# Eight of eleven down projection steps by seven products instead of seven, with smaller scratch

## The chip, the cores and the metric

The kernel runs on one core of a Trainium2 chip. The time is device microseconds of one execution. Engines are named as in the profile: PE (TensorE matmul), PEld (its weight loads), DVE (VectorE), ACT (ScalarE), POOL (GpSimd) and SP (SyncE, which here only issues DMAs).

## The reference

One decoder layer on 272 positions (16 meta tokens and 256 tokens) of width 2048, float32:

```python
h = h + concat(retention_heads, mlstm_heads) @ w_out
u = rmsnorm(h, norm_ffn)
up = causal_dwconv(u @ w_up, ffn_conv_w, ffn_conv_b)      # 2 x 5632 wide, 3 taps
gate, val = split(up, [FFN_DIM])
h = h + (silu(gate) * val) @ w_down                       # 5632 x 2048
out = rmsnorm(h, norm_final)[:, N_META:]
```

The change lies in the last product, `(silu(gate) * val) @ w_down`, and in what is prepared for it.

## The kernel before

**Precision.** Every large product is taken in three matmuls: an operand x is kept as hi = x rounded to fp32r and lo = x - hi, and hi*hi + lo*hi + hi*lo are summed in PSUM. For a weight tile this means a DMA into a `wraw` buffer (4 of them), a cast on ACT into `whi` and a subtraction on DVE into `wlo` (5 each; `load_w`, L114 to L124).

**Stages in time.** Input projections and the two kinds of heads; `w_out` (L630 to L638); then twice (two halves of the FFN rows) an up projection and a down projection. An up projection makes 22 pairs of 128-row tiles (gate and value), each by `project`, `conv3`, Silu and a multiplication (L770 to L788). The 22 tiles of a half are 11 steps of the down projection, two tiles each.

**Down projection.** Per half it runs two blocks, `b` = 0 and 2 (L915): output columns of strips b and b+1, 512 each. A block has four PSUM sums `cs[tt, j]` (token half tt, strip j; pool `at`, four buffers) and four more, `ps` (pool `mm`, four buffers).

- A *plain* step (`product`, L813) loads both strips' weights and makes 2 strips x 2 token halves x 2 row tiles x 3 = 24 matmuls of 512 columns.
- A *fast* step (`seven`, L833) treats the step as a 2x2 block product (activation blocks A11, A12, A21, A22 by row tile and token half; weight blocks B11 to B22 by row tile and strip) and makes seven products of 3 matmuls, 21, by Winograd's form of Strassen's scheme. The activation sums S1 to S4 are made on POOL in the up stage (L802 to L805), the weight sums in `seven` and earlier. Seven steps of eleven are fast: `FAST` (L593); in the last block of all, the two in `BOTH` are plain.

**Weight sums.** One of them, T2 = B22 - B12 + B11, is made in advance for each fast step: class `Early` (L599) loads three 512-wide weight blocks on POOL's queue into a home, two DVE sums follow some projections later (L615, L616), and the result goes to DRAM (`kept`, L617). `seven` then loads it (L840) with three blocks from `wd7` (L841) into one of two raw places in `hT` (`left`, in turn), makes two more sums (L844, L845; their results take `wraw` buffers) and casts and splits four groups. `wd7` is a copy of the weights in the order in which `seven` wants them.

**Ends of a block.** After the last fast step `share` (L877 on) turns the four `ps` into four x tiles and adds each to `hn` in SBUF by an accumulating DMA from POOL's queue (`onto`, L878). After the last step the four `cs` are copied by ACT into x tiles (L951) and sent the same way. x tiles are slices of `x5`, which has five; the copies use 4, 3, 1, 0 and `share` uses 0 to 3. `seven` of the next block's first fast step casts only behind the last of these copies (`emptied`). In the last block the sums are added to `hn` by DVE instead (`add`), with an order of steps of its own, and four plain steps of strip 3 are kept for the end.

**Order.** Within an engine instructions run in program order, which a planner makes from the order of emission, its own estimates of time and the `issue_after` rules. An engine, and SP's queue of DMA issues too, stands still while its next instruction waits for a semaphore.

The two lines on which the ends of a block turn:

```python
x6, x7, x5, x1 = (x_tile(i) for i in range(4))          # share
x = x_tile((4, 3, 1, 0)[2 * j + n])                     # copies of cs
```

Of the kernel before, what the change touches and what calls it, by code (L numbers as in the profile page):

```python
# [83 lines left out]
def trunk(ctx: ExitStack, tc: tile.TileContext, io, out: bass.AP):  # L84
    nc = tc.nc
# [5 lines left out]
    wpool = ctx.enter_context(pool("wpool", 1, side="left"))  # L91
# [501 lines left out]
    FAST = [1, 2, 3, 5, 6, 7, 8]  # L593
# [5 lines left out]
    class Early:  # L599


        def __init__(self, b, q, home, after, pace=None):

            self.home, self.age = home, 0
            self.kept = dram.tile([P, 512], F32, name=f"kept{b}_{q % NQD}", bufs=1)
# [6 lines left out]
        def finish(self, after):  # L612
            t = self.home[:, 0, :]
            with tc.issue_after(after.ins):
                nc.vector.tensor_tensor(out=t, in0=self.home[:, 1, :], in1=t, op=ALU.subtract)  # L615
            nc.vector.tensor_tensor(out=t, in0=self.home[:, 2, :], in1=t, op=ALU.add)  # L616
            nc.gpsimd.dma_start(self.kept, t)  # L617

    early, running = {}, []
    ahead = [(0, q) for q in FAST[:5]]  # L620
# [3 lines left out]
    begins = [1, 4, 6, 8, 10]  # L624
# [39 lines left out]
    x5 = midp.tile([P, 5, 512], F32, name="x5")  # L664
    pace = midp.tile([P, 1], F32, name="pace")

    def x_tile(i):
        return x5[:, i, :]
# [8 lines left out]
    def conv3(ps, f, name):  # L677
# [3 lines left out]
        o = wk2.tile([P, SEQ], F32, name=name)  # L681
# [62 lines left out]
    for half in range(2):  # L744
        units = [(b, q) for b in (0, 2) for q in FAST if (half, b) != (1, 2) or q not in BOTH]
        homes = [left[0][:, 0:3, :], left[1][:, 0:3, :], x5[:, 1:4, :]]
        if half == 0:
            units = units[len(ahead):]
            begins = [2 + 4 * i for i in range(9)]
            homes = 9 * [homes[2]]  # L750
# [18 lines left out]
        for jj in range(NHF):  # L769
# [27 lines left out]
            else:  # L797
# [5 lines left out]
                nc.gpsimd.tensor_tensor(out=sums[:, S3, :], in0=e11, in1=e21, op=ALU.subtract)  # L803
# [28 lines left out]
        def seven(b, q, cs, ps, first, last, after, norm):  # L832
# [7 lines left out]
            nc.sync.dma_start(raw[:, 0, :], early[b, q])  # L840
            nc.sync.dma_start(raw[:, 1:4, :], io["wd7"][b // 2, half * NQD + q][:, 1:4, :])  # L841
            ta, tb = (wpool.tile([P, 2, 512], F32, name="wraw", bufs=4) for _ in range(2))

            nc.vector.tensor_tensor(out=ta, in0=raw[:, 0:1, :].to_broadcast([P, 2, 512]), in1=raw[:, 1:3, :], op=ALU.subtract)  # L844
            nc.vector.tensor_tensor(out=tb[:, 0, :], in0=raw[:, 3, :], in1=raw[:, 0, :], op=ALU.subtract)  # L845
            copied = None
            for w, to in (
                (raw[:, 2:4, :], ((S4, cs[0, 1], False, False), (A12, cs[0, 0], False, False))),
                (raw[:, 0:2, :], ((S2, ps[2], first, last), (A11, ps[0], first, last))),
                (ta, ((S3, ps[1], first, last), (S1, ps[3], first, last))),  # L850
                (tb[:, 0:1, :], ((A22, cs[1, 0], False, False),)),
# [217 lines left out]
```

## Time and profile before

| what | value |
| --- | --- |
| median of 3 runs | 1207.14 us (1205.92 to 1208.45) |
| the profiled execution, its own time | 1207.7 us |
| its span, first to last instruction | 1205.9 us |
| granted PE clock | 0.999 |
| down projection, first half | about 718 to 833 us of the span |
| down projection, second half | about 1084 us to the end |

The profile has a page of fixed parts (busy time by engine, the span in 40 slices, DMA queues, the chain of work that ended last) and views that answer to questions: busy time by stage, groups of instructions by line, instructions in order of time with the idle time before them and what ended it, and DMA issues in a stretch with their median time to landing. In a row such as `wlo<-wraw,whi 128x1024` the names are the program's tiles, with out before the arrow.

### The profile page before, as it was taken

To read this page: it belongs to the slowest core of one execution; us is meant where nothing else is said; L and a number is where in the kernel's file an instruction comes from. 1 tells how busy PE (TensorE), PEld (TensorE's weight loads), DVE (VectorE), ACT (ScalarE), POOL (GpSimd) and SP (SyncE) were. 2 spreads that over 40 slices of the span, in tenths; PEclk is the share of its full clock that TensorE was granted. 3 is DMA by queue.
4 is the path that set the end of the run, shared out by engine and by line. 5 is a ranking of instruction groups with operands and counts; after the bars stand their busy time and mean duration, and the time that the engine had idled before them with its cause. 6 is when DMAs were issued, how large, how long until landed. Compare 5 with 4: busy or idle time off the path is not lost.

```text
span 1205.9 us, 22794 instructions
## 1 busy us (share of the span) xinstructions
PE 1194.6 (99%) x8956; PEld 1151.2 (95%) x8956; DVE 971.5 (81%) x1444; ACT 709.5 (59%) x963; POOL 162.8 (14%) x223
## 2 busy tenths in 40 slices
PE   9999999999999999999999999999999999999997
PEld 9999999999999999999999998878999999998886
DVE  8968788766775966789889879897788778789897
ACT  8747656655656646555555557664555555556664
POOL 0100001111110311021122100202022112100232
PEclk9999999999999999999999999999999999999999
DMA  8765555666565965766766834959787777755956
GB/s 278 269 212 164 170 184 170 197 183 192 169 192 165 349 200 175 252 220 212 253 219 214 279 117 175 278 177 276 284 251 255 223 240 249 261 176 211 274 181 186
DMA packets 83004, 263.27 MB, mean 218 GB/s; under 512 B 14672, under 2 KB 18896, under 8 KB 82768
## 3 DMA queue, kind: packets, MB, share of 16 engines
q1 hardware_dynamic: 71952, 223.85, 57.0%
q0 software_dynamic: 10368, 37.11, 10.1%
q8 instruction: 70, 1.15, 0.4%
q10 hardware_dynamic: 576, 0.85, 0.2%
q14 instruction: 38, 0.31, 0.1%
HBM read 243.42 MB, written 11.27 MB: 211 GB/s over the span
## 4 chain that ended last, share of the span: by engine, by line
PE 96%; DMA 2%; DVE 1%; ACT 0%; issue 0%; SPq 0%; DVEq 0%; ACTq 0%
PE mmps L130 26%; PE mmps L131 25%; PE mmps L133 25%; PE atps L827 2%; PE atps L828 2%; PE atps L830 2%; PE mmps L860 2%; PE mmps L862 2%; PE mmps L859 2%; PE atps L862 1%; PE atps L860 1%; PE atps L859 1%; DMA hn<-x 1%; PE atps L379 1%; DMA hT<-in_wd 1%; PE atps L371 0%
## 5 line engine op out<-in xcount | busy, mean ns | idle before, releaser
L121 ACT CAST whi<-wraw 128x1024 fp32r<-128x1024 f32 x352 | 369.3, 1050 | 342.0 <-PE mmps L131 228.7
L123 DVE TENSOR_TENSOR wlo<-wraw,whi 128x1024 fp32r<-128x1024 f32 x352 | 432.3, 1230 | 72.5 <-ACT whi L121 70.0
L130 PE MATMUL mmps<-uh,whi 128*128 128x258 f32 x1408 | 346.1, 283 | 0.0
L131 PE MATMUL mmps<-ul,whi 128*128 128x258 f32 x1408 | 346.0, 283 | 0.0
L130 PEld LDWEIGHTS mmps<-uh,whi 128*128 128x128 f32 x1408 | 267.6, 190 | 0.1
L131 PEld LDWEIGHTS mmps<-ul,whi 128*128 128x128 f32 x1408 | 267.1, 190 | 0.1
L130 PE MATMUL mmps<-xh,whi 128*128 128x272 f32 (+2 forms) x864 | 219.8, 288 | 0.0
L131 PE MATMUL mmps<-xl,whi 128*128 128x272 f32 (+2 forms) x864 | 218.3, 286 | 0.0
L133 PE MATMUL mmps<-uh,wlo 128*128 128x258 f32 x1408 | 196.5, 282 | 0.0
L133 PEld LDWEIGHTS mmps<-uh,wlo 128*128 128x128 f32 x1408 | 179.9, 189 | 0.0
L131 PEld LDWEIGHTS mmps<-xl,whi 128*128 128x128 f32 x864 | 162.8, 188 | 0.0
L130 PEld LDWEIGHTS mmps<-xh,whi 128*128 128x128 f32 x864 | 162.5, 188 | 0.1
L133 PE MATMUL mmps<-xh,wlo 128*128 128x272 f32 (+2 forms) x864 | 126.7, 285 | 0.0
L133 PEld LDWEIGHTS mmps<-xh,wlo 128*128 128x128 f32 x864 | 114.2, 188 | 0.0
L680 DVE TENSOR_TENSOR cu<-mmps,rstd 128x258 f32<-128x258 f32 x88 | 37.4, 425 | 55.3 <-PE mmps L133 54.8
L764 ACT CAST whi<-hT 128x1024 fp32r<-128x1024 f32 x52 | 53.6, 1052 | 27.2 <-PE atps L828 7.3
L766 DVE TENSOR_TENSOR wlo<-hT,whi 128x1024 fp32r<-128x1024 f32 x52 | 62.1, 1220 | 4.9 <-ACT whi L764 3.7
L131 PE MATMUL mmps<-mixl,whi 128*128 128x258 f32 x256 | 63.0, 283 | 0.0
L130 PE MATMUL mmps<-mixh,whi 128*128 128x258 f32 x256 | 62.4, 282 | 0.0
L764 ACT CAST whi<-wraw 128x1024 fp32r<-128x1024 f32 (+1 forms) x52 | 43.0, 838 | 16.8 <-PE mmps L860 6.8
L766 DVE TENSOR_TENSOR wlo<-wraw,whi 128x1024 fp32r<-128x1024 f32 (+1 forms) x52 | 52.2, 1037 | 0.6 <-PE mmps L862 0.2
L827 PE MATMUL atps<-whi,mh 128*128 128x512 f32 (+1 forms) x132 | 50.9, 387 | 1.3 <-ACT whi L121 1.1
(280 smaller groups left out, 1700.1 us busy)
## 6 DMA issues: line engine op xcount, KB each, us to landing
wraw<-in_wu SPq DMA_DIRECT2D x176, 512.0 KB, 4.4
wraw<-in_wi SPq DMA_DIRECT2D x108, 512.0 KB, 4.1
hT<-in_wd SPq DMA_DIRECT2D x26, 768.0 KB, 4.7
wraw<-in_wd SPq DMA_DIRECT2D x36, 512.0 KB, 4.7
wraw<-in_wo SPq DMA_DIRECT2D x32, 512.0 KB, 4.2
x<-in_wd POOLq DMA_DIRECT2D x13, 768.0 KB, 7.0
hn<-x POOLq DMA_DIRECT2D x27, 256.0 KB, 7.9
hT<-kept SPq DMA_DIRECT2D x26, 256.0 KB, 2.9
```

Source lines behind the costliest of these rows:

```text
L121: nc.scalar.copy(hi, raw)
L123: nc.vector.tensor_tensor(out=lo, in0=raw, in1=hi.bitcast(F32), op=ALU.subtract)
L130: nc.tensor.matmul(ps, hi[:, k, :], xh(kk), start=kk == first, stop=False)
L131: nc.tensor.matmul(ps, hi[:, k, :], xl(kk), start=False, stop=False)
L133: nc.tensor.matmul(ps, lo[:, k, :], xh(kk), start=False, stop=kk == last)
L680: evacuated = nc.vector.tensor_tensor(out=u, in0=ps[:, :NQ], in1=rstd2, op=ALU.mult)
L764: copied = nc.scalar.copy(hi, x)
L766: return copied, nc.vector.tensor_tensor(out=lo, in0=x, in1=hi.bitcast(F32), op=ALU.subtract)
L827: nc.tensor.matmul(ps, ah[i], hi[:, i, cols], start=first and i == 0, stop=False)
L859: nc.tensor.matmul(o, sh[:, f, m, :], hi[:, i, :], start=begin, stop=False)
L860: nc.tensor.matmul(o, sl[:, f, m, :], hi[:, i, :], start=False, stop=False)
L862: nc.tensor.matmul(o, sh[:, f, m, :], lo[:, i, :], start=False, stop=end)
```

## The change

- `FAST` gets eight steps (1, 2, 3, 4, 6, 7, 8, 9) instead of seven (1, 2, 3, 5, 6, 7, 8); plain are 0, 5 and 10. In the last block `BOTH` is now 8 and 9, so six steps are fast there instead of five, in another order.
- Both early weight sums, B11 - B12 and B22 + B11 - B12, are stored (`kept` becomes two blocks wide). `seven` loads both, two blocks of `wd7` and, by a third DMA, one block into a `wraw` buffer. One DVE sum of 1024 columns is left; S3 changes its sign, and the products are grouped in another order. `wd7` is laid out anew.
- `x5` has four x tiles instead of five; the copies of `cs` use 3, 1, 0, 2. `vt` has one buffer instead of two.
- More early units: six instead of five in the `w_out` stage, ten instead of nine in half 0, fourteen instead of twelve in half 1.

```diff
-    FAST = [1, 2, 3, 5, 6, 7, 8]
+    FAST = [1, 2, 3, 4, 6, 7, 8, 9]
...
-            self.kept = dram.tile([P, 512], F32, name=f"kept{b}_{q % NQD}", bufs=1)
+            self.kept = dram.tile([P, 2, 512], F32, name=f"kept{b}_{q % NQD}", bufs=1)
...
-            t = self.home[:, 0, :]
+            t1, t2, b11 = (self.home[:, i, :] for i in range(3))
             with tc.issue_after(after.ins):
-                nc.vector.tensor_tensor(out=t, in0=self.home[:, 1, :], in1=t, op=ALU.subtract)
-            nc.vector.tensor_tensor(out=t, in0=self.home[:, 2, :], in1=t, op=ALU.add)
-            nc.gpsimd.dma_start(self.kept, t)
+                nc.vector.tensor_tensor(out=t1, in0=b11, in1=t1, op=ALU.subtract)
+            nc.vector.tensor_tensor(out=t2, in0=t2, in1=t1, op=ALU.add)
+            nc.gpsimd.dma_start(self.kept, self.home[:, 0:2, :])
...
-    ahead = [(0, q) for q in FAST[:5]]
+    ahead = [(0, q) for q in FAST[:6]]
...
-    begins = [1, 4, 6, 8, 10]
+    begins = [1, 3, 5, 7, 9, 11]
...
-    x5 = midp.tile([P, 5, 512], F32, name="x5")
+    x5 = midp.tile([P, 4, 512], F32, name="x5")
...
-        o = wk2.tile([P, SEQ], F32, name=name)
+        o = wk2.tile([P, SEQ], F32, name=name, bufs=2 if name == "gt" else 1)
...
-            begins = [2 + 4 * i for i in range(9)]
-            homes = 9 * [homes[2]]
+            begins = [2 + 4 * i for i in range(10)]
+            homes = 10 * [homes[2]]
...
-                nc.gpsimd.tensor_tensor(out=sums[:, S3, :], in0=e11, in1=e21, op=ALU.subtract)
+                nc.gpsimd.tensor_tensor(out=sums[:, S3, :], in0=e21, in1=e11, op=ALU.subtract)
...
-            nc.sync.dma_start(raw[:, 0, :], early[b, q])
-            nc.sync.dma_start(raw[:, 1:4, :], io["wd7"][b // 2, half * NQD + q][:, 1:4, :])
-            ta, tb = (wpool.tile([P, 2, 512], F32, name="wraw", bufs=4) for _ in range(2))
-
-            nc.vector.tensor_tensor(out=ta, in0=raw[:, 0:1, :].to_broadcast([P, 2, 512]), in1=raw[:, 1:3, :], op=ALU.subtract)
-            nc.vector.tensor_tensor(out=tb[:, 0, :], in0=raw[:, 3, :], in1=raw[:, 0, :], op=ALU.subtract)
+            w = io["wd7"][b // 2, half * NQD + q]
+            nc.sync.dma_start(raw[:, 0:2, :], early[b, q])
+            nc.sync.dma_start(raw[:, 2:4, :], w[:, 2:4, :])
+            b22, ta = (wpool.tile([P, 2, 512], F32, name="wraw", bufs=4) for _ in range(2))
+            nc.sync.dma_start(b22[:, 0, :], w[:, 1, :])
+
+            nc.vector.tensor_tensor(out=ta, in0=raw[:, 2:4, :], in1=raw[:, 1:2, :].to_broadcast([P, 2, 512]), op=ALU.subtract)
...
-                (raw[:, 2:4, :], ((S4, cs[0, 1], False, False), (A12, cs[0, 0], False, False))),
-                (raw[:, 0:2, :], ((S2, ps[2], first, last), (A11, ps[0], first, last))),
-                (ta, ((S3, ps[1], first, last), (S1, ps[3], first, last))),
-                (tb[:, 0:1, :], ((A22, cs[1, 0], False, False),)),
+                (raw[:, 2:4, :], ((A11, ps[0], first, last), (A12, cs[0, 0], False, False))),
+                (raw[:, 0:2, :], ((S1, ps[3], first, last), (S2, ps[2], first, last))),
+                (b22[:, 0:1, :], ((S4, cs[0, 1], False, False),)),
+                (ta, ((S3, ps[1], first, last), (A22, cs[1, 0], False, False))),
...
-            steps = [0, 1, 4, 2, 7, 3, 5, 6, 8, 9, 10] if final else range(NQD)
+            steps = [0, 1, 5, 2, 8, 3, 4, 6, 7, 9, 10] if final else range(NQD)
...
-                        x = x_tile((4, 3, 1, 0)[2 * j + n])
+                        x = x_tile((3, 1, 0, 2)[2 * j + n])
...
-    a["wd7"] = np.ascontiguousarray(np.stack([pairs[:, 1, :, :, 0], pairs[:, 0, :, :, 0], pairs[:, 1, :, :, 1], pairs[:, 0, :, :, 1]], 3))
+    a["wd7"] = np.ascontiguousarray(np.stack([pairs[:, 1, :, :, 0], pairs[:, 1, :, :, 1], pairs[:, 0, :, :, 0], pairs[:, 0, :, :, 1]], 3))
```

More of the change, by code (lines that the diff above doesn't have):

```diff
@@ L867, in seven @@
                         squares(*g)
-                reached = nc.gpsimd.tensor_tensor(out=junk[:, 0:1], in0=tb[:, 0, 0:1], in1=tb[:, 0, 0:1], op=ALU.add)
+                reached = nc.gpsimd.tensor_tensor(out=junk[:, 0:1], in0=ta[:, 0, 0:1], in1=ta[:, 0, 0:1], op=ALU.add)
                 with tc.issue_after(reached.ins):
```

## The prediction

> **What bounds the kernel now.** I read the page first: which engine is busy, whether its clock is granted, and what the chain that ended last is made of.
>
> ```profile
> span 1205.9 us, 22794 instructions
> PE 1194.6 (99%) x8956; PEld 1151.2 (95%) x8956; DVE 971.5 (81%) x1444; ACT 709.5 (59%) x963; POOL 162.8 (14%) x223
> PEclk9999999999999999999999999999999999999999
> PE 96%; DMA 2%; DVE 1%; ACT 0%; issue 0%; SPq 0%; DVEq 0%; ACTq 0%
> ```
>
> TensorE (PE) works from end to end at full clock, and 96% of the chain is PE. So a matmul that goes is worth its own time, and an edit elsewhere is worth nothing unless it makes PE wait. Next the busy times by stage: two stretches of the up projection, then three of the four blocks of the down projection (a block is a pair of 512-column output strips in one half of the FFN rows).
>
> ```profile
> 470.00:716.00 246.00, 246.00 (x2053) 245.94 (x2053) 210.83 (x321) 135.70 (x183) 39.22 (x55) 1.00 0.68 221
> 833.00:1084.00 251.00, 251.00 (x2096) 251.00 (x2095) 199.98 (x298) 138.65 (x188) 40.95 (x68) 1.00 0.75 245
> 718.00:776.00 58.00, 58.00 (x256) 47.64 (x255) 52.84 (x57) 35.90 (x42) 5.75 (x7) 1.00 0.68 220
> 776.00:833.00 57.00, 55.90 (x250) 45.48 (x249) 49.18 (x52) 33.90 (x39) 4.78 (x6) 1.00 0.71 212
> 1085.00:1140.00 55.00, 55.00 (x241) 44.82 (x239) 49.85 (x54) 34.16 (x38) 3.74 (x5) 1.00 0.73 242
> ```
>
> Columns: sum, then PE, PEld, DVE, ACT, POOL busy, clock, DMA share, GB/s. PE fills every stage, but in the down projection DVE is at 91% (52.84 of 58.00) and DMA at 68 to 73%. PE's waits there are few. The order of time on PE shows the three that matter:
>
> ```profile
> 793.62 0.50 PE L827 MATMUL atps<-whi,mh 128*128 128x512 f32 x1 [0.45 <-ACT whi L121]
> 819.27 0.51 PE L827 MATMUL atps<-whi,mh 128*128 128x512 f32 x1 [0.65 <-ACT whi L121]
> 1140.19 0.50 PE L827 MATMUL atps<-whi,mh 128*128 128x512 f32 x1 [0.16 <-ACT x L951]
> ```
>
> The first two are plain steps behind several seven-product steps, short of cast weights. The third is the change of block: PE waits for the copy (L951) that empties the last block's sums. About 0.3 us are lost there, since the matmul before began at 1138.96 and four of them take 0.9.
>
> **The change, part by part.** *Matmuls.* A plain step is 24 matmuls of 512 columns, a fast one 21. One step per block turns fast (in the last block too: six instead of five), so 4 x 3 = 12 go. From the row 718 to 776, 58.00 us / 256 = 0.227; the other PE-filled row gives 55.00 / 241 = 0.228. 12 x 0.228 = **-2.7 us**. That is all that can be gained in PE work.
>
> *The cover at the end of a block.* Before, two plain steps (9 and 10) follow the last fast step (8); after, the last fast step is 9 and one plain step follows. In that time two things must happen: `share` forms four x tiles and sends them by accumulating DMAs (L878), and the weights of the next block's step 0 must come in. Here is the change of block in half 1, on PE, ACT and POOL:
>
> ```profile
> 1129.11 0.62 PE L862 MATMUL mmps<-wlo,sh 128*128 128x512 f32 x2
> 1138.96 1.07 PE L830 MATMUL atps<-wlo,mh 128*128 128x512 f32 x4
> ...
> 1136.03 1.05 ACT L121 CAST whi<-wraw 128x1024 fp32r<-128x1024 f32 x1 [1.54 <-DMA wraw<-in_wd]
> 1138.60 1.05 ACT L121 CAST whi<-wraw 128x1024 fp32r<-128x1024 f32 x1 [1.53 <-DMA wraw<-in_wd]
> 1139.56 2.04 ACT L951 COPY x<-atps 128x512 f32<-128x512 f32 x4
> ...
> 1129.28 0.88 POOL L878 DMA_DIRECT2D hn<-x  x1 [44.04 <-ACT x L884]
> 1132.69 1.20 POOL L878 DMA_DIRECT2D hn<-x  x1
> ```
>
> Call T the end of the last product sum, 1129.11 + 0.62 = 1129.73. PE has work of the old block until 1140.03, so the cover is 10.3 us. One plain step less takes 24 x 0.228 = 5.5 of it: 4.8 are left. What must fit in:
>
> ```profile
> 1128.33 10.35 SPq L118 DMA_DIRECT2D wraw<-in_wd  x3
> ...
> wraw<-in_wd SPq DMA_DIRECT2D x2, 512.0 KB, 8.3
> hn<-x POOLq DMA_DIRECT2D x4, 256.0 KB, 8.4
> hn<-x POOLq DMA_DIRECT2D x1, 256.0 KB, 9.2
> hn<-x POOLq DMA_DIRECT2D x4, 256.0 KB, 5.4
> ```
>
> (SP's issue of step 0's two weight loads; then time to landing: of these two, of the four share DMAs, of the last of these alone, and, in half 0, of the four that carry the emptied sums away.)
>
> First, x tiles. Before there are five, and the first copy of L951 goes into one that `share` does not use (4). After there are four, `share` uses all, and the copies take them in order 3, 1, 0, 2: each copy waits until the share DMA that reads its tile has landed. The last one lands at 1132.69 + 9.2 = 1141.9, T + 12.2. In the new order of products two sums (ps 2 and 3) are ready a group earlier, so I allow 0.5 us: T + 11.7. Behind it stand a copy (2.04 / 4 = 0.5) and the last product of step 0 (6 x 0.228 = 1.4): step 0 ends at T + 13.6, while without waiting it would end at T + 4.8 + 5.5 = 10.3. Wait 3.3 us. Behind the waiting copy on ACT stand the casts of the next fast step, so PE has nothing else to do. Second, weights: step 0's loads take the slots that the last fast step frees, thus leave at T or just before, and the casts that wait for them end at 1137.08 and 1139.65, T + 7.4 and T + 9.9. PE wants the first at T + 4.8: wait 2.6 us, unless the copies hold it longer. The two run side by side, so I take **3.0 us** for one change of block; bounds 0 (landings as in the last row) and 4.
>
> It happens at three places. The change of block in half 0 has T = 763.61 and nearly the same last landing:
>
> ```profile
> 762.99 0.62 PE L862 MATMUL mmps<-wlo,sh 128*128 128x512 f32 x2
> ...
> hn<-x POOLq DMA_DIRECT2D x1, 256.0 KB, 8.1
> ```
>
> So +3.0 in each half, less the 0.3 lost in half 1 now. From half 0 to half 1's up projection PE needs no emptied sum, but it needs weights:
>
> ```profile
> 820.32 0.62 PE L862 MATMUL mmps<-wlo,sh 128*128 128x512 f32 x2
> 826.12 1.05 ACT L121 CAST whi<-wraw 128x1024 fp32r<-128x1024 f32 x1 [1.74 <-DMA wraw<-in_wu]
> 830.16 0.28 PE L130 MATMUL mmps<-uh,whi 128*128 128x258 f32 x1
> wraw<-in_wu SPq DMA_DIRECT2D x4, 512.0 KB, 7.3
> ```
>
> T = 820.94; up-projection matmuls begin at T + 9.2 now, at T + 3.7 with one plain step less, plus about 0.9 for four old matmuls done later (L830); their first cast ends at T + 6.2: **+1.7 us**. Bounds 0 and 5 (the four copies stand in ACT's queue there too).
>
> [...]
>
> *Edits that I cost at nothing.*
>
> ```profile
> L844 DVE TENSOR_TENSOR wraw<-hT 128x1024 f32<-128x1024 f32 x26 | 31.7, 1220 | 5.6 <-DMA hT<-in_wd 5.5
> L845 DVE TENSOR_TENSOR wraw<-hT 128x512 f32<-128x512 f32 x26 | 17.8, 685 | 0.1
> L766 DVE TENSOR_TENSOR wlo<-hT,whi 128x1024 fp32r<-128x1024 f32 x52 | 62.1, 1220 | 4.9 <-ACT whi L764 3.7 <-PE atps L862 0.7 <-issue 0.2
> L123 DVE TENSOR_TENSOR wlo<-wraw,whi 128x1024 fp32r<-128x1024 f32 x352 | 432.3, 1230 | 72.5 <-ACT whi L121 70.0 <-PE atps L862 0.4
> L615 DVE TENSOR_TENSOR x<-x 128x512 f32<-128x512 f32 x13 | 8.9, 685 | 1.5 <-DMA x<-in_wd 1.5
> L682 ACT ACTIVATE vt<-cu,par 128x256 f32<-128x256 f32 x44 | 26.5, 602 | 13.7 <-DVE cu L680 13.3
> ```
>
> A fast step loses its 512-wide DVE sum (L845, 0.69 us). DVE per block of 11 steps: before, 7 fast (three 1.22, one 0.69, L844 1.22, L845 0.69 = 6.3) and 4 plain (2 x 1.23) make 53.6 us; after, 8 x 5.6 and 3 x 2.5 make 51.9, against PE's 240 x 0.228 = 54.7. DVE stays under PE, so nothing follows, unless four fast steps in a row outrun it: a fast step is 21 x 0.228 = 4.8 us of PE and 5.6 of DVE, and a plain step gives 3.0 back. SP issues three DMAs per fast step (1.25 MB instead of 1.0), and the third waits for a weight slot, with the next step's loads behind it; the slot is freed at most two DVE operations (1.9 us) after the raw slot that the loads wait for anyway. 30 early units instead of 26 add four times two DVE sums of 0.69 and two DMA issues on POOL, one of them of twice the bytes, in stretches where PE is full and DVE has 35 us spare of 246; landing late, one would hold a fast step. Each half has one fast pair more to prepare (POOL sums, casts): the same cover. One `vt` buffer: L682 writes it after `cu` of its own pair, which already waits for PE, while the old `vt` was read about a projection before. The sign of S3 and the new layout of `wd7` change no count. In the last block 12 matmuls fewer stand between `share` and the end; 0 to +1.5, taken at 0, since PE is full up to its last matmuls.
>
> **Sum.** -2.7 - 0.3 + 3.0 + 3.0 + 1.7 = +4.7. The profiled execution took 1207.7 us (span 1205.9 and 1.8 around it), so 1212.4; it lies 0.6 above the median 1207.14: **1211.8 us**.
>
> **The rivals.** *Not slower: landings get short (0.19).* With one plain step less, a megabyte less is asked for at once around T. If the share DMAs and loads land in 5.4 and 4.2 us (the load row below), the last x tile is free at about T + 8 and waits stay under half a microsecond: 1207.14 - 2.7 - 0.3 = 1204.1. The point is a landing of about 5.5 us from issue. [...]
>
> ```profile
> wraw<-in_wd SPq DMA_DIRECT2D x2, 512.0 KB, 4.2
> ```
>
> [...]
>
> *In between (0.18).* Landings of 6.5 to 7 us: 1 us at each of three places, 1207.1.
>
> *DMA binds the seven-product steps as well (0.11).* A quarter more bytes on 73% share: then each of seven rows of four such steps ends like the waits at 793.62 and 819.27 (0.45 and 0.65, say 0.6 us): 1211.8 + 4.2 = 1216.0. Against it: DVE's chain per fast step gets shorter.
>
> *The forecast (0.52).*
>
> **How the numbers follow.** What this kernel's measurement tells from no change is about 0.2%, 2.4 us: 1204.7 to 1209.6. Faster 0.18 (the first rival but for 0.01), same 0.25 (0.01, the second, and 0.06 of the forecast, waits of some 2 us), slower 0.57. The range goes from half a microsecond below the first rival to just above the third, 1203.6 to 1217.0; outside lie deeper gains by the two early waits and stacked waits.
>
> **What would show it.** Right: 8944 matmuls; L951's copies in half 1 some 12 us after the last product sum, with the DMA `hn<-x` as releaser; PE gaps of 2 to 4 us at both changes of block, and ACT casts waiting on `in_wu` behind half 0. Wrong: PE full across these places (first rival), or gaps among the seven-product steps, ended by `in_wd`, `kept` or DVE (third).

## The result and the profile after

| | before | after |
|---|---|---|
| median | 1207.8 us | **1238.2 us** |
| runs | 1205.9 to 1209.5 (4) | 1237.3 to 1242.3 (4) |
| ratio, 95% interval | | **1.0256 (1.0232 to 1.0281)**: slower |
| profiled execution, its span | 1207.7, 1205.9 | 1238.6, 1236.8 |

The change costs 30 us where 4.7 were forecast: the sign was right, the size off by a factor of more than six. The page of the changed kernel, the same lines as before:

```profile
span 1236.8 us, 22906 instructions
PE 1205.9 (98%) x8944; PEld 1152.4 (93%) x8944; DVE 970.2 (78%) x1440; ACT 711.6 (58%) x973; POOL 190.7 (15%) x242
PEclk9999999999999999999999999999999999989899
DMA 3%; DVE 1%; ACT 1%; POOL 1%; PE 1%; issue 1%; SPq 0%; DVEq 0%; ACTq 0%
```

The 12 matmuls are gone (8956 to 8944), and yet PE shows more busy time, since its clock drops in the last slices (0.94 and 0.84 of full speed in the last two rows below) and matmuls there take longer. PE was 96% of the chain that ended last; now the chain that is followed back stays short and runs through DMA, DVE, ACT and POOL. The stages (columns as before: sum, PE, PEld, DVE, ACT, POOL busy, clock, DMA share, GB/s):

```profile
470.00:716.00 246.00, 246.00 (x2053) 245.94 (x2053) 211.40 (x321) 135.23 (x183) 44.69 (x62) 1.00 0.71 238
718.00:776.00 58.00, 55.56 (x241) 44.64 (x239) 48.97 (x52) 34.61 (x38) 1.85 (x3) 1.00 0.70 231
776.00:834.00 58.00, 56.75 (x238) 45.96 (x239) 48.77 (x48) 37.67 (x43) 6.04 (x7) 0.97 0.80 233
1089.00:1149.00 60.00, 53.06 (x212) 40.21 (x212) 47.56 (x53) 33.43 (x40) 0.92 (x2) 0.94 0.65 223
1149.00:1171.00 22.00, 17.25 (x62) 12.83 (x62) 11.51 (x13) 10.28 (x14) 6.99 (x8) 0.84 0.96 244
```

The up projection is as full as it was (246.00 of 246.00, the same 2053 matmuls). Nearly all of the loss is in the down projection: 212 matmuls in 60 us, or 62 in 22, where 60 us of full work hold 263.

To place it I sum, over the matmul records, what passes from one start to the next beyond the length at full clock (the median from start to start in the trace of before: 0.229 us for 512 columns, 0.120 for 258): PE time lost by waiting and by a lower clock. In us:

| | half 0 block 1 | change of block | block 2 | half 1's up | start of down | block 1 | change of block | last block | sum |
|---|---|---|---|---|---|---|---|---|---|
| before | 0.0 | 0.0 | 1.7 | 0.2 | 0.0 | 0.0 | 0.4 | 0.1 | 2.6 |
| after | 1.0 | 5.0 | 1.0 | 1.4 | 8.1 | 4.3 | 7.6 | 6.7 | 34.9 |

Check: 34.9 - 2.6 lost, -2.7 for 12 matmuls, +1.5 behind the last matmul (8.5 us before, 10.0 after) makes 31.1; the spans differ by 30.9. So there are four large places; the forecast had the two changes of block, at 3.0 each. (Every row of this table and of the one further down comes from one execution; its places, rounded singly, add up to within 0.2 of its sum.)

**The change of block in half 1**, ACT, then DVE, POOL and PE:

```profile
1157.37 1.04 ACT L121 CAST whi<-wraw 128x1024 fp32r<-128x1024 f32 x1 [5.10 <-DMA wraw<-in_wd]
1159.17 1.04 ACT L121 CAST whi<-wraw 128x1024 fp32r<-128x1024 f32 x1 [0.75 <-DMA wraw<-in_wd]
1160.19 0.58 ACT L952 COPY x<-atps 128x512 f32<-128x512 f32 x1
1161.85 0.58 ACT L952 COPY x<-atps 128x512 f32<-128x512 f32 x1 [1.08 <-DMA hn<-x]
1165.77 0.58 ACT L952 COPY x<-atps 128x512 f32<-128x512 f32 x1 [3.33 <-DMA hn<-x]
1167.10 0.59 ACT L952 COPY x<-atps 128x512 f32<-128x512 f32 x1 [0.74 <-DMA hn<-x]
...
1154.70 0.68 DVE L888 TENSOR_TENSOR x<-mmps,x 128x512 f32<-128x512 f32 x1
1158.45 1.23 DVE L123 TENSOR_TENSOR wlo<-wraw,whi 128x1024 fp32r<-128x1024 f32 x1 [3.07 <-ACT whi L121]
1159.59 0.68 DVE L890 TENSOR_TENSOR x<-x,mmps 128x512 f32<-128x512 f32 x1
1160.19 0.68 DVE L896 TENSOR_TENSOR x<-x,mmps 128x512 f32<-128x512 f32 x1
...
1160.80 3.50 POOL L879 DMA_DIRECT2D hn<-x  x4 [4.24 <-issue]
...
1160.83 0.80 PE L827 MATMUL atps<-whi,mh 128*128 128x512 f32 x1 [4.50 <-ACT x L952]
1161.42 0.63 PE L828 MATMUL atps<-whi,ml 128*128 128x512 f32 x1
1161.85 0.63 PE L827 MATMUL atps<-whi,mh 128*128 128x512 f32 x1
```

Read it in order. Step 0's weights come late: ACT's cast stands 5.10 us for them. The first weights are cast by 1158.41, but PE is released only by the first copy (L952, from 1160.19), which stands on ACT behind the cast of the second weights. On DVE the low part of these weights (L123) stands in program order ahead of the last two sums of `share` (L890, L896), which could have followed the sum before them (L888, ended at 1155.38). So these sums are some 4 us late, and the last share DMAs leave POOL only at 1160.80. The third and fourth copy (L952) wait for just these DMAs (3.33 and 0.74 us). PE, idle for 4.50 us, then starts a matmul every 0.43 us (1161.42 to 1161.85) instead of 0.23. Weights, share and copies thus stand **in series**, and PE pays for its idle time a second time through its clock, which stands at 0.50 from 1159.43 to 1166.25.

**The start of half 1's down projection**, SP, then POOL, DVE and PE:

```profile
1087.94 0.33 SPq L844 DMA_DIRECT2D wraw<-in_wd  x1
1093.15 0.33 SPq L841 DMA_DIRECT2D hT<-kept  x1
...
1088.81 0.58 POOL L617 DMA_DIRECT2D kept<-hT  x1 [7.66 <-DVE hT L616]
...
1099.78 1.23 DVE L846 TENSOR_TENSOR wraw<-hT 128x1024 f32<-128x1024 f32 x1 [5.03 <-DMA hT<-kept]
...
1101.99 0.79 PE L863 MATMUL atps<-wlo,sh 128*128 128x512 f32 x1 [4.19 <-DVE wlo L766]
```

SP stands from 1087.94 to 1093.15 ahead of a load of the early sums. Of half 1's 14 early units the last (the list `begins`, L752: begun at projection 40) has its home in `left[1]`, one of the two places into which the down projection's steps load. Its 512 KB left for DRAM only at 1088.81 (POOL L617), and the place is free when they have landed, 4.3 us later, at 1093.1. Before, with 12 units, the last one had its home in `x5`, and the last use of `left[1]` began at projection 36.

**The last block**, POOL, DVE and SP, and then POOL of the kernel before:

```profile
1176.07 10.43 POOL L869 TENSOR_TENSOR junk<-wraw 128x1 f32<-128x1 f32 x1 [6.17 <-ACT junk L694]
...
1183.49 1.22 DVE L846 TENSOR_TENSOR wraw<-hT 128x1024 f32<-128x1024 f32 x1
1184.63 1.82 DVE L766 TENSOR_TENSOR wlo<-wraw,whi 128x512 fp32r<-128x512 f32 x2
1188.23 2.01 DVE L766 TENSOR_TENSOR wlo<-hT,whi 128x1024 fp32r<-128x1024 f32 x1 [1.78 <-PE atps L861]
...
1177.33 0.33 SPq L841 DMA_DIRECT2D hT<-kept  x1
1186.53 0.33 SPq L844 DMA_DIRECT2D wraw<-in_wd  x1
```

```profile
1162.52 0.34 POOL L868 TENSOR_TENSOR junk<-wraw 128x1 f32<-128x1 f32 x1 [6.01 <-ACT junk L694]
```

An addition of one element per partition (`reached`, L869 after, L868 before), put there only to set an order, takes 10.43 us instead of 0.34. It reads `ta`, which lies in a weight slot, so the slot stays taken and the third load of SP (L844) leaves 9.2 us after the one ahead of it.

### The profile page after: what moved, and what is told of

Same layout as the page of the kernel before. It is cut to its first block, busy times and chain, and to the rows that moved or that the text cites. A ratio compares the mean times of both kernels' runs of the same rounds, so it can differ in the third digit from the quotient of the medians.

```text
span 1236.8 us, 22906 instructions
## 1 busy us (share of the span) xinstructions
PE 1205.9 (98%) x8944; PEld 1152.4 (93%) x8944; DVE 970.2 (78%) x1440; ACT 711.6 (58%) x973; POOL 190.7 (15%) x242
## 5 line engine op out<-in xcount | busy, mean ns | idle before, releaser
L121 ACT CAST whi<-wraw 128x1024 fp32r<-128x1024 f32 x344 | 359.2, 1047 | 284.7 <-PE mmps L131 158.4
L123 DVE TENSOR_TENSOR wlo<-wraw,whi 128x1024 fp32r<-128x1024 f32 x344 | 425.2, 1237 | 69.6 <-ACT whi L121 68.7
L130 PE MATMUL mmps<-uh,whi 128*128 128x258 f32 x1408 | 346.2, 283 | 0.2 <-ACT whi L121 0.2
L130 PEld LDWEIGHTS mmps<-uh,whi 128*128 128x128 f32 x1408 | 267.7, 190 | 0.4 <-ACT whi L121 0.4
L130 PE MATMUL mmps<-xh,whi 128*128 128x272 f32 (+2 forms) x864 | 220.0, 288 | 0.0
L130 PEld LDWEIGHTS mmps<-xh,whi 128*128 128x128 f32 x864 | 162.7, 188 | 0.1
L766 DVE TENSOR_TENSOR wlo<-hT,whi 128x1024 fp32r<-128x1024 f32 x60 | 72.2, 1232 | 13.0 <-ACT whi L764 11.0
L764 ACT CAST whi<-hT 128x1024 fp32r<-128x1024 f32 x60 | 61.8, 1050 | 15.1 <-DMA hT<-kept 3.7
L130 PE MATMUL mmps<-mixh,whi 128*128 128x258 f32 x256 | 62.4, 283 | 0.0
L764 ACT CAST whi<-wraw 128x512 fp32r<-128x512 f32 (+1 forms) x60 | 48.8, 836 | 19.3 <-DVE wlo L766 8.8
L879 POOL DMA_DIRECT2D hn<-x x27 | 23.6, 1006 | 221.0 <-ACT x L885 185.0
L846 DVE TENSOR_TENSOR wraw<-hT 128x1024 f32<-128x1024 f32 x30 | 38.1, 1270 | 23.2 <-DMA hT<-kept 23.1
L766 DVE TENSOR_TENSOR wlo<-wraw,whi 128x512 fp32r<-128x512 f32 (+1 forms) x60 | 55.0, 951 | 1.3 <-ACT whi L764 1.3
```

The source lines that it names most:

```text
L121: nc.scalar.copy(hi, raw)
L123: nc.vector.tensor_tensor(out=lo, in0=raw, in1=hi.bitcast(F32), op=ALU.subtract)
L130: nc.tensor.matmul(ps, hi[:, k, :], xh(kk), start=kk == first, stop=False)
L764: copied = nc.scalar.copy(hi, x)
L766: return copied, nc.vector.tensor_tensor(out=lo, in0=x, in1=hi.bitcast(F32), op=ALU.subtract)
L846: nc.vector.tensor_tensor(out=ta, in0=raw[:, 2:4, :], in1=raw[:, 1:2, :].to_broadcast([P, 2, 512]), op=ALU.subtract)
```

## The experiments

The theory at this point: one plain step too few behind the last seven-product step, weights and share DMAs in series, and two accidents (home, `reached`). The rivals: the 256 KB more that each step reads, the smaller scratch, and the sum `ta`, which the new layout takes first. Each diff is against the changed kernel unless it says otherwise.

**e1: another order of the homes, so that the last unit lies in `x5`.**

```diff
-        homes = [left[0][:, 0:3, :], left[1][:, 0:3, :], x5[:, 1:4, :]]
+        homes = [left[0][:, 0:3, :], x5[:, 1:4, :], left[1][:, 0:3, :]]
...
-            homes = 10 * [homes[2]]
+            homes = 10 * [homes[1]]
```

> Edit: in half 1 the second and third home of the early units change places, so the last of the 14 units (begun at projection 40) uses the x tiles and no longer one of the two raw places that the down projection loads into. Theory (each loss of the changed kernel has its own place and cause): the 8.1 us that PE loses at the start of half 1's down projection (about 1101 to 1109 us) go, total about 1229 to 1231 us; the change of block (7.6 us lost) and the last block (6.7) stay. Rival (the seven-product steps are short of DMA or DVE throughput throughout, 1.25 MB instead of 1.0 MB each): the loss only moves to the next steps, total 1235 or more.

**e3: without the one-element addition.** (Five x tiles beside eight such steps, which would have been e2, do not fit into SBUF: their pool needs 80.2 KB per partition, and 79 are left.)

```diff
-                reached = nc.gpsimd.tensor_tensor(out=junk[:, 0:1], in0=ta[:, 0, 0:1], in1=ta[:, 0, 0:1], op=ALU.add)
-                with tc.issue_after(reached.ins):
+                with tc.issue_after(copied.ins):
```

> Edit: the POOL addition that reads one element of a weight buffer (reached, L869) is left out; POOL's gain multiplications follow the casts in order alone. It computes nothing that the output needs. Theory: SP no longer stands still from 1177.7 to 1186.5 us behind the buffer that this addition holds, and of the 6.7 us lost in the last block 4 to 5 go: about 1233. Rival (the last block is short of weights for throughput): 1237 or more, SP waiting elsewhere.

Measured, one execution each beside 1207.2 of before: e1 1237.5, e3 1238.7. The places answer as the theory has it (start of the down projection 8.1 to 2.7; last block 6.7 to 3.6), the totals do not move: the first block of half 0, where neither edit changes an instruction, lost 5.9 and 4.1 instead of 1.0. The instructions of that block and their order are the same in all three, so one execution of these kernels cannot tell 3 to 5 us, neither in its total nor at one place of a table. Later ones were timed in rounds.

**e4: seven such steps again, new layout and small scratch kept.**

```diff
-    FAST = [1, 2, 3, 4, 6, 7, 8, 9]
+    FAST = [1, 2, 3, 5, 6, 7, 8]
...
-    ahead = [(0, q) for q in FAST[:6]]
+    ahead = [(0, q) for q in FAST[:5]]
...
-            steps = [0, 1, 5, 2, 8, 3, 4, 6, 7, 9, 10] if final else range(NQD)
+            steps = [0, 1, 4, 2, 7, 3, 5, 6, 8, 9, 10] if final else range(NQD)
```

> Edit: the old choice of seven steps of eleven, with its order of steps and its number of early units, on the new layout (both sums from DRAM, three loads a step, four x tiles, one vt buffer). Theory: two plain steps stand again behind the last seven-product step, the last early unit is in the x tiles, so only the x tiles' wait is left, 1 to 2 us at each change of block: 1208 to 1211. Rival (throughput: each such step loads 1.25 MB and DVE waits for kept): 1215 or more.

Measured, one execution: 1214.4 beside 1207.2. Most of the loss goes with the eighth step, but 7 us stay with the layout or the scratch.

**e5, e6, e8: the sum `ta` later** (taken when its own products are due, behind the second group; e5 with eight such steps, e6 with seven, e8 with the edits of e1 and e3 as well).

```diff
-            nc.vector.tensor_tensor(out=ta, in0=raw[:, 2:4, :], in1=raw[:, 1:2, :].to_broadcast([P, 2, 512]), op=ALU.subtract)
...
+                if g == 3:
+                    with tc.issue_after(second.ins):
+                        nc.vector.tensor_tensor(out=ta, in0=raw[:, 2:4, :], in1=raw[:, 1:2, :].to_broadcast([P, 2, 512]), op=ALU.subtract)
```

> Edit: in every seven-product step the DVE sum ta is issued behind the second group's split of the same step, instead of ahead of all splits; the arithmetic is the same. Theory (a chain through SP and DVE): DVE waits with the next step's ta for the landing of kept, ahead of the splits that free the raw place, so the next kept load leaves only then, and such steps come every 7.2 to 8.2 us where PE needs 4.8. With ta behind the splits the chain is broken: kept loads every 5 to 6 us within a run, PE's losses inside the blocks nearly gone, those at the changes of block left: 1238 falls to 1215 to 1222 us. Rival (bytes: 1.25 MB a step are too much for the DMA engines): still over 7 us a step, 1235 or more.

> Edit: the old choice of seven steps on the new layout, with ta behind the second split as in e5. Theory: the 4.9 us lost in half 0's second block and some of the last block's go: 1207 to 1210 us. Rival (bytes): as without the edit, 1214.

> Edit: the changed kernel with ta behind the second split, the home order of e1 and without the POOL addition of e3. Theory: 5 us or more below e5 alone, from the start of half 1's down projection and the last block: 1210 to 1217 us. Rival: no better than e5.

Measured: e5 1232.8, e6 1216.8, e8 1231.2 beside 1207.3. With seven steps nothing is won (1214.4 before the edit), so the theory that the loss comes through `ta` at the head of each step fell. e5 and e8 win 5 to 7 us in single executions, and were not followed up.

**e7: the kernel before with eight such steps and the small scratch, but its own layout** (one early sum in DRAM, 1.0 MB a step; against the kernel before).

```diff
-    FAST = [1, 2, 3, 5, 6, 7, 8]
+    FAST = [1, 2, 3, 4, 6, 7, 8, 9]
...
-    x5 = midp.tile([P, 5, 512], F32, name="x5")
+    x5 = midp.tile([P, 4, 512], F32, name="x5")
...
-                        x = x_tile((4, 3, 1, 0)[2 * j + n])
+                        x = x_tile((3, 1, 0, 2)[2 * j + n])
```

> Edit: the old layout (one early sum in DRAM, two loads a step, two DVE sums in the step) with the eight steps, four x tiles and one vt buffer of the changed kernel. Theory (the new layout's chain through kept makes most of the loss): the steps come every 5 to 6.5 us as before, and the changes of block lose 3 to 5 us each for want of cover: 1212 to 1220 us. Rival (eight steps of eleven are too many for any layout: DVE needs 6.3 us for a step of 4.8 us on PE): 1225 or more.

Measured: 1239.7, with losses at the places of the changed kernel (6.2 and 7.0 at the changes of block, 9.5 at the start of half 1's down projection, 6.3 in the last block). The loss does not need the new layout. It does not follow that the layout is free: DVE's work per step is larger in e7, as e13 shows.

The next four were timed in rounds beside one set of 13 runs of before (median 1207.0).

**e9: share's sums ahead of step 0's weights on DVE.**

```diff
-                            share(ps, b, final)
+                            shared = share(ps, b, final)
...
-                    w = load_step(b + j, q)
+                    with tc.issue_after(shared.ins) if b == 2 and q == 0 else nullcontext():
+                        w = load_step(b + j, q)
```

> The changed kernel, but the low part of step 0's weights (L123) stands on DVE behind share's last sum (L896) instead of ahead of its last two sums. In the changed kernel's trace those two sums ran at 1159.59 and 1160.19, behind a L123 that waited for weights landed at 1157.29, though their inputs were there at about 1155.4 and the sum before them ended at 1155.4; so the last two share DMAs left 4.5 us late. Theory (in series: late weights, then the x tiles): the loss at half 1's change of block falls from 7.6 to 3 to 5 us and at half 0's from 5.0 to 3 to 4; total 3 to 5 us less than the changed kernel, about 1234. Rival (side by side: PE would wait for the late weights in any case, and the x tiles only fill the same time): the sums run early, the copies' waits for hn<-x shrink, but PE's wait only moves from the copies to the weights, and both changes of block keep their 5 and 7.6 within a microsecond; 1238.

Measured: 1232.1 (1228.7 to 1233.0; ratio 1.0201, 1.0173 to 1.0229). Half 1's change of block 7.6 to 5.4, half 0's the same (4.9). In series, then, in half 1; but the order on DVE is only part of it. Of the 6 us of the total these are 2.2; the last block, whose order the edit leaves as it was, lost 2.9 instead of 6.7 in this execution.

**e10: two plain steps behind the last seven-product step again**, at the price of eight in a row.

```diff
-            steps = [0, 1, 5, 2, 8, 3, 4, 6, 7, 9, 10] if final else range(NQD)
+            steps = [0, 1, 5, 2, 8, 3, 4, 6, 7, 9, 10] if final else [0, 1, 2, 3, 4, 6, 7, 8, 9, 5, 10]
```

> The changed kernel with the order 0, 1, 2, 3, 4, 6, 7, 8, 9, 5, 10 in the three blocks that are not the last: again two plain steps stand behind the last seven-product step, at the price of eight such steps in a row. Theory (the missing plain step at the block's end): the losses at the changes of block fall from 5.0 and 7.6 to under 1 and under 3 us, and up1 from 1.4 to 0.2; total 8 to 10 less than the changed kernel, about 1229. Rival (five such steps in a row do not hold: DMA at 70 per cent and DVE at 5.6 us of work against 4.8 us of matmuls): what is won there is lost again inside the blocks, at the sixth to eighth step of the row, 2 to 4 us in each of three blocks; total 1234 to 1241.

Measured: **1223.2** (1218.6 to 1226.4; ratio 1.0129, 1.0098 to 1.0161), 15 us less than the changed kernel, from moving one step. The changes of block fall to 0.0 and 1.0, the last block, whose order stays as it was, to 3.6. The rival holds too: block 2 of half 0 now loses 4.5.

**e11: the edits of e1, e3, e9 and e10 together.**

> The changed kernel with four edits: the homes' order of e1, no one-element addition on POOL (e3), two plain steps behind the last seven-product step (e10), share's sums ahead of step 0's weights (e9). If the causes found are all of it and do not stand in for each other: start of half 1's down projection 2.7 instead of 8.1, last block 3.6 instead of 6.7, changes of block under 1 and under 3 instead of 5.0 and 7.6: 1238.2 less 18 is 1220. Rival (what is mended at one place comes back at the next, as in e1 and e3, whose totals did not move): 1228 to 1238.

Measured: 1221.3 (1218.2 to 1223.8; ratio 1.0115, 1.0091 to 1.0140), near the first expectation. Changes of block 0.1 and 0.0, start of the down projection 2.5, last block 1.7, but 3.0, 4.5 and 5.8 inside the three other blocks. Here is one of them, with its DMA share of 0.81, and what PE waited for in the whole execution (us in total, times, longest):

```profile
776.00:834.00 58.00, 55.34 (x236) 43.24 (x235) 49.95 (x49) 37.76 (x44) 6.92 (x8) 1.00 0.81 242
```

```profile
PE atps L827 <- ACT whi L121: 4.3, 5, 1.6
PE mmps L863 <- DVE wlo L766: 4.1, 5, 1.3
```

**e12: the small scratch alone in the kernel before** (the last two edits of e7's diff and one `vt` buffer).

> The kernel before (seven seven-product steps, first early weight sum in DRAM, its layout) with the smaller scratch of the change alone: four x tiles, emptied in the order 3, 1, 0, 2, and one vt buffer. e4 (new layout and smaller scratch, seven steps) was 7.2 us over the kernel before. Theory (the scratch costs it: the x tiles make the copies at a change of block wait): 1 to 3 us at the two changes of block and up to as much in the block behind each, 1210 to 1215. Rival (the new bytes cost it: both sums read back, 1.25 MB a step): nothing here, 1207 to 1208.

Measured: 1207.5 (10 runs; ratio 1.0005, 0.9996 to 1.0015). With two plain steps behind the last product, four x tiles and one `vt` buffer cost nothing that can be measured. So e4's 7 us are the layout's.

**e13: e11's four edits in the old layout** (on e7). **e14 and e15: e4 and e11 without reading the second early sum back**.

```diff
-            nc.sync.dma_start(raw[:, 0:2, :], early[b, q])
+            nc.sync.dma_start(raw[:, 0:1, :], early[b, q][:, 0:1, :])
```

> Eight seven-product steps in the layout of before (one early sum in DRAM, 1.0 MB a step in two DMAs, one 512-wide DVE sum more), with the four edits of e11. Theory (the 14 us that e11 has left are the layout's: more bytes a step, DMA at 73 to 81 per cent, waits on hT<-kept): the losses inside the blocks fall from 3.0, 4.5 and 5.8 to under 1 each, and the kernel takes 1206 to 1211, at best 2 us under the kernel before. Rival (eight such steps in a row outrun DVE and DMA whatever the layout): 1216 to 1224, with DVE, whose work a step grows to 6.3 us, as what PE waits for.

> e4 (seven seven-product steps, new layout) with the second early sum not read back: it is written to DRAM, but the read takes 256 KB instead of 512, and the place of the second sum holds old data, so two of the seven products are left wrong. Same instructions but for the bytes; three DMAs a step, and the third still waits for its weight slot. Theory (bytes): total 1207 to 1209, as before. Rival (the third DMA and its slot on SP hold the next step's loads, or DVE's order): 1213 to 1215, as e4's 1214.4.

> e11 with the same 256 KB a step not read back (the second early sum's place holds old data). Theory (bytes): the losses inside the blocks fall by half or more, 1209 to 1214. Rival (the third DMA and its slot, or the row of eight): 1219 to 1222, as e11's 1221.3.

Measured, beside 1207.1 (16 runs): e14 **1208.0** (ratio 1.0007, 0.9997 to 1.0016), e15 1212.4 (1.0035, 1.0018 to 1.0052), e13 1224.4 (1.0148, 1.0126 to 1.0169). With 256 KB a step less, and the same three DMAs and slots, the 7 us of the layout are gone: it is the bytes of that read (by one execution of e4, and ten of e14). What PE waited for in e4, and below it all that it waited for in e14 (L199 and L130 belong to the start of the kernel; e4 has the wait of L199 too):

```profile
PE mmps L863 <- DVE wlo L766: 1.8, 3, 0.8
PE atps L827 <- ACT whi L121: 1.4, 3, 1.0
...
PE atps L827 <- ACT x L952: 1.0, 1, 1.0
```

```profile
PE atps L199 <- DVE ones L171: 1.2, 1, 1.2
PE atps L130 <- ACT whi L224: 0.6, 1, 0.6
PE atps L830 <- DVE wlo L123: 0.4, 1, 0.4
```

The theory fell for e13, which loses 2.7, 2.0 and 7.2 in the three blocks: the old layout reads less, but has the 512-wide sum on DVE, and eight such steps in a row leave DVE hardly any room. A stretch of e13:

```profile
776.00:834.00 58.00, 56.89 (x250) 45.48 (x249) 55.22 (x57) 38.31 (x45) 6.82 (x9) 1.00 0.69 208
```

DVE is busy for 55.22 of 58 us (e11: 49.95), DMA at 0.69 (e11: 0.81). e15 reads as many bytes a step as e13 (1.0 MB) without that sum, and is 12 us faster (its grouping of the products and its third DMA differ too); e11 differs from e15 by the 256 KB alone, and is 9 us slower. So with the old layout DVE binds such a row, with the new one the load of the early sums.

**e16: the changed kernel with e14's edit. e17: the kernel before with one plain step instead of two behind the last seven-product step, nothing else. e18: e17 with the small scratch.** e17's diff, against the kernel before:

```diff
-            steps = [0, 1, 4, 2, 7, 3, 5, 6, 8, 9, 10] if final else range(NQD)
+            steps = [0, 1, 4, 2, 7, 3, 5, 6, 8, 9, 10] if final else [0, 1, 2, 3, 4, 9, 5, 6, 7, 8, 10]
```

> The changed kernel with the second early sum not read back (256 KB a step less; its place holds old data). If bytes and missing plain step cost each its own price, the changes of block keep most of their 5.0 and 7.6 and the total falls by about 9, to 1229. If the stalls at the changes of block are the bytes' own doing, they fall to 1 to 2 us each and the total to 1216 to 1222, as with two plain steps. If the single plain step alone decides, 1235 or more.

> The kernel before with the order 0, 1, 2, 3, 4, 9, 5, 6, 7, 8, 10 in the three blocks that are not the last: one plain step instead of two behind the last seven-product step, nothing else changed (seven such steps, 1.0 MB a step, five x tiles). By the prediction's own terms: weights late by 2.6 us at each change of block and 1.7 us at the way into half 1's up projection, so 1213 to 1214. If late weights and late x tiles add up: here the first copy has a free tile, so still 2 to 4 a change, 1212 to 1216. If the stall needs the bytes and the eighth step as well: under 1 us a place, 1207 to 1209.

> e17 with the smaller scratch (four x tiles, one vt buffer), which alone cost nothing in e12. If the x tiles matter once only one plain step stands behind the last product: 2 to 4 us more than e17, at the two changes of block, with copies that wait for hn<-x. If the late weights alone decide, as much as e17 within 1 us.

Measured, beside 1207.7 (6 runs): e16 1222.2 (ratio 1.0120, 1.0098 to 1.0142); e17 **1221.7** (1.0112, 1.0084 to 1.0140); e18 **1227.6** (1.0165, 1.0141 to 1.0190). e17 beats every expectation upwards: one step moved, not a byte or an instruction more, costs 14 us. The x tiles, free in e12, cost 5.8 more here. e16 loses 3.1 and 8.0 at the changes of block, so these stalls do not need the bytes; what the bytes' edit wins there is the start of the down projection (8.1 to 0.1), the blocks, and half of the last one, each by one execution.

PE time lost, in us, as in the table above:

| | half 0 block 1 | change | block 2 | half 1's up | start of down | block 1 | change | last block | sum |
|---|---|---|---|---|---|---|---|---|---|
| e12 small scratch | 0.0 | 1.1 | 1.0 | 0.2 | 0.0 | 0.0 | 0.1 | 0.6 | 2.9 |
| e17 one plain step | 0.0 | 4.3 | 1.5 | 0.1 | 0.0 | 0.0 | 6.9 | 3.5 | 16.5 |
| e18 both | 0.1 | 6.5 | 1.1 | 0.3 | 0.0 | 0.0 | 7.3 | 5.7 | 21.1 |
| after | 1.0 | 5.0 | 1.0 | 1.4 | 8.1 | 4.3 | 7.6 | 6.7 | 34.9 |
| e10 two plain again | 1.3 | 0.0 | 4.5 | 2.2 | 7.9 | 3.1 | 1.0 | 3.6 | 23.8 |
| e11 all four | 3.1 | 0.1 | 4.5 | 0.2 | 2.5 | 5.8 | 0.0 | 1.7 | 17.8 |
| e15 and fewer bytes | 0.0 | 0.0 | 1.7 | 1.3 | 2.3 | 0.6 | 0.9 | 3.8 | 10.6 |

No version here beats the kernel before; e15 shows that even without the bytes the eighth step loses 8 us (10.6 - 2.6) against the 2.7 that it wins. What makes up e15's rest was not tried.

## Why the prediction was wrong

e17 is the prediction's own central step alone, so its trace shows what the sum lacked. Half 1's change of block, ACT, then DVE, POOL and PE, then two windows:

```profile
1143.33 1.05 ACT L121 CAST whi<-wraw 128x1024 fp32r<-128x1024 f32 x1 [4.19 <-DMA wraw<-in_wd]
1145.20 1.04 ACT L121 CAST whi<-wraw 128x1024 fp32r<-128x1024 f32 x1 [0.83 <-DMA wraw<-in_wd]
1146.15 1.06 ACT L951 COPY x<-atps 128x512 f32<-128x512 f32 x2
1147.45 0.59 ACT L951 COPY x<-atps 128x512 f32<-128x512 f32 x1 [0.23 <-DMA hn<-x]
1154.06 0.58 ACT L951 COPY x<-atps 128x512 f32<-128x512 f32 x1 [6.02 <-DMA hn<-x]
...
1144.41 1.22 DVE L123 TENSOR_TENSOR wlo<-wraw,whi 128x1024 fp32r<-128x1024 f32 x1 [1.55 <-ACT whi L121]
1145.55 0.68 DVE L889 TENSOR_TENSOR x<-x,mmps 128x512 f32<-128x512 f32 x1
...
1147.03 3.50 POOL L878 DMA_DIRECT2D hn<-x  x4 [2.99 <-DVE x L895]
...
1146.79 0.50 PE L827 MATMUL atps<-whi,mh 128*128 128x512 f32 x1 [2.81 <-ACT x L951]
1154.70 0.58 PE L827 MATMUL atps<-whi,mh 128*128 128x512 f32 x1 [1.91 <-ACT x L951]
```

```profile
1148.15:1151.56 3.41, 3.41 (x10) 2.67 (x9) 0.00 (x0) 0.00 (x0) 2.38 (x3) 0.50 0.99 228
1154.98:1158.39 3.41, 3.41 (x9) 2.65 (x9) 2.77 (x3) 3.41 (x5) 1.23 (x2) 0.50 1.02 183
```

Columns of the windows as before; the third number from the end is PE's granted clock. From 1144 to 1160 PE loses 8.5 us here (the table counts the end of it with the last block), in three parts.

1. **The late weights: 3.0 us.** The cast of step 0's first weights waits 4.19 us for its DMA, and PE starts at 1146.79, 3.2 us after its last start instead of 0.2. That is the size that the prediction forecast for the whole change of block, but not its way: the first weights are cast by 1144.38, and what releases PE is the first copy (L951), which stands on ACT behind the late casts of both weights. The copies ahead of these casts were not tried.
2. **The last copy: 2.1 us.** The fourth copy waits 6.02 us for `hn<-x`, and PE waits again (1154.70). This is the series seen above in the changed kernel: late weights, the sums of `share` behind them on DVE (L889 runs at 1145.55, behind L123), the share DMA behind the sums (1147.03), the copy behind the DMA.
3. **The clock: 3.4 us**, the rest. PE's clock was at 0.50 from 1148.15 to 1151.56, soon after its first wait, and from 1154.98 to 1158.39, around the end of its second.

In this third part a matmul of 512 columns takes 0.43 us from start to start against 0.23 before, for 3.41 us each time, and the waits beside it are of 2.81 and 1.91 us.

The other traces of this case say how often. In the changed kernel the clock falls at the three waits that cost PE 3.20, 4.36 and 4.67 us (to 0.50 for 3.41, 6.83 and 6.83 us), and not at one of 1.76. Counted over the traces, from 500 us of the span on, up to the last matmul, the clock falls to 0.50 for 3.41 us, or two or three times that, at 17 of the 18 waits that cost PE 2.8 us or more (from start to start, less the matmul's own 0.229), at 10 of the 15 that cost 1.75 to 2.8, and at no shorter one. So a wait just under 2 us (1.91 in e17) was enough here, and what decides is open.

Now the prediction, by its steps.

- **Matmuls, -2.7: right.** 8944, and a full-clock spacing of 0.229.
- **Change of block, 3.0 each: the first failed step.** "The two run side by side, so I take 3.0 us for one change of block." They run in series, since ACT and DVE work in order: a late weight (ACT waits 4.19 us for it in e17, 5.10 in the changed kernel) holds the copies on ACT and the sums on DVE, and these hold the DMAs that free the x tiles (the last copy of e17 waits 6.02 us for one). The two changes lost 5.0 and 7.6. e9 undoes one link, the order on DVE, and wins 2.2 us at half 1's change. In the changed kernel the copies start at T + 8.7 to T + 15.6 (T is 1151.5); the prediction had the last of them free to start at T + 11.7. Three waited for the reason it named, `hn<-x`; but the landings were shorter than the 9.2 us it took, and the issues later (DMA issues of the changed kernel from 1148 to 1163):

```profile
hn<-x POOLq DMA_DIRECT2D x6, 256.0 KB, 6.2
```

- **The x tiles inside that step.** They are not hidden beside the weights: 5.8 us on top (e18 against e17, with one `vt` buffer as well), and nothing with two plain steps (e12). The cover decides whether they cost.
- **Into half 1's up projection, +1.7: wrong, and near the number by luck.** (Its own figures give 1.6.) The changed kernel lost 1.4 us in that projection against 0.2, but nothing at the crossing, between 820 and 890 us of the span, for which the term stood: the losses lie at 894, 901 and 999. With one plain step and the old bytes the projection lost 0.1 (e17), and with one plain step and the bytes not read 0.1 (e16). So the missing step is not their cause. Nor are the bytes alone: e15 lost 1.3 there without them, e11 0.2 with them. The cause stays open.
- **"Edits that I cost at nothing": the other failed step.** The start of half 1's down projection and the last block lost 8.1 and 6.7, more than the two changes of block together. The scratch by itself: right. The early units: the sentence "landing late, one would hold a fast step" was the 8.1 us at the start of half 1's down projection, costed at nothing because the up projection around the units was full; not asked was which place the last of them lies in. The other homes bring it to 2.7 (e1) and 2.5 (e11), and the bytes not read alone bring it to 0.1 (e16). With the other homes and the bytes not read 2.3 are left (e15), so what the late unit costs by itself is not settled. The third DMA and the bytes: the third DMA costs nothing (e14), the bytes do. The last block, "taken at 0": 6.7, and its cause stays open in part (it lost 3.6 in e3, but also 2.9 and 3.6 in e9 and e10, which do not touch it).
- **The rivals.** That landings get short (0.19) came half true (6.2 us) and did not help, as the transfers start later; the landings of 6.5 to 7 us of the next rival (0.18), for which it had 1207.1, are about those of e17 (6.5 in that change of block), which took 1221.7. That DMA binds (0.11, 4.2 us) is the right mechanism for what the layout costs with seven such steps: 6.4 us, e4's 1214.4 against e14's 1208.0; in the changed kernel 16 go with the bytes (e16).
- **The range** ended at 1217.0, with "stacked waits" left outside, and stacked waits are what came. Every term was a first wait; none stood for what a late load does next: hold an engine's queue (ACT's for 4.19 us in e17), and through PE's wait lower the clock (to 0.50 for 3.41 us, twice).

From before to after, by medians: one plain step less +14.0 (1207.7 to 1221.7, e17), the small scratch on top +5.8 (e18), and +10.6 to 1238.2 for the eighth step with its early units and the bytes, the 2.7 won already taken off. Backwards, the second plain step returns 15.0 (e10), and the bytes 16.0 (e16). The prices overlap (the last two alone make 31.0 of 30.4): the parts taken alone must not be added. Left open are e11's and e15's rest, and why e17's last block still loses some 2 us after the clock is back.

## What to carry to other kernels

A full engine with one plain step of spare work behind its hard steps is not the same as one with two: price the cover itself, by what must land within it, before the matmuls that go. Do not set two late arrivals side by side until the in-order queues are read: ask of each late load what stands behind its first reader on that engine. And where TensorE waits for some 3 us, look at the clock that follows: here it was mostly 3.41 us at half speed, so 1.7 us more, and twice that or more behind the six waits that cost over 4 us.

## What was not expected of the hardware

- An addition of one element per partition on GpSimd took 10.43 us (1176.07 to 1186.50) and ended as VectorE came to its first gap of that stretch (its operations of 1183.49 and 1184.63 follow each other up to 1186.45, the next starts at 1188.23). Before, the same addition took 0.34. What held it was not shown. Its price is not settled: without the addition the last block lost 3.6 us instead of 6.7 (e3), but e9 and e10 lost 2.9 and 3.6 with it in place.
- The mean DMA share did not tell here when DMA binds. In the stretch from 776 to 834, e4 (first row) loses 3.05 of 58 us on PE at a share of 0.74, and e14, with 256 KB a step less, loses nothing at 0.75, nor from 1089 to 1149 at 0.80:

```profile
776.00:834.00 58.00, 54.95 (x234) 42.92 (x233) 46.13 (x46) 35.89 (x40) 4.36 (x6) 1.00 0.74 231
776.00:834.00 58.00, 58.00 (x273) 48.30 (x272) 47.96 (x47) 36.77 (x42) 5.25 (x7) 1.00 0.75 228
```

- A wait of TensorE of 2.81 us (e17) was followed by 3.41 us at half clock, and so cost half as much again (1.7 us beside 3.0); one of 1.91 us was followed by 3.41 us of it too.
